# Moving the softmax division of two attention mixers from the probabilities to the stored outputs, and letting high-part splits run on GpSimd or ScalarE

## The chip, the cores and the metric

The kernel runs on one core of a Trainium2 chip. The metric is the device time of one execution in microseconds (us). A core has TensorE (PE in the rows, with its weight loads as PEld), VectorE (DVE), ScalarE (ACT), GpSimd (POOL) and SyncE (SP), which issues all transfers of this kernel.

## What is computed

A trunk of two layers on one sequence of 1024 tokens, width 1024, in float32. Each layer:

```python
h = rmsnorm(x, ln1_g[layer]);  proj = h @ w_in[layer]          # 2464 columns
out_a = mixer_dilated(...)   # A: 6 heads of 64, three dilated windows, softmax
out_b = mixer_mla(...)       # B: 6 heads of 64 (query/key 96), low-rank q and kv, softmax
out_c = mixer_diff(...)      # C: 4 heads, softmax1 - lambda * softmax2, sub-norm
x = x + concat([out_a, out_b, out_c]) @ w_o[layer]
x = x + square(relu(rmsnorm(x, ln2_g[layer]) @ w_up[layer])) @ w_down[layer]
# after both layers: rmsnorm(x, final_g)
```

In each head of A and B, `p = softmax(scores + mask)` over the keys and `out = p @ v`. All attention is causal.

## The kernel before

**Precision.** Every product of two float32 tensors is made of three TensorE products: each operand is split into a high part (`hi`, a rounded copy) and a low part (`lo`, the operand minus its high part), and high*high, high*low and low*high are summed in PSUM (`mm3`). The high part is a copy: `hi_pool` (kind `hi`, from SBUF) or `hi_act` (kind `hiact`, from PSUM). The low part is a subtraction (`lo_dve`, `lo_pool`).

**The scheduler.** The program is not written in the order in which it runs. Every instruction is noted by `Recorder`, and `order` then runs a list scheduler over the notes with costs in ns for each engine; each engine gets its instructions in the order that this planner found, and works through them strictly in that order. Tiles come from tags with a fixed number of slots (`SLOTS`; `'pp'` has 5, `'ms'`, `'mx'` and `'oo'` have 2 each), and an instruction is planned when a slot is free. Where `WAYS` names several letters for a kind of work (v VectorE, s ScalarE, g GpSimd), the planner picks the engine. All instructions of the kernel carry the line of the replay loop (L418), so in the rows the tile names tell them apart.

**The attention of a layer.** There are 16 heads in the order A0, C0, C1, A1, A2 (two heads each) and then six heads of B. `scores` handles 8 blocks of 128 queries of a head: TensorE makes the scores (`s_A`, `s_B`), VectorE adds the mask and takes the row maximum (`p_A`, with the maximum in `w_A`), ScalarE takes the exponential in place and its row sum, and for A and B

```python
nc.vector.reciprocal(w[:, 3:4], tot)     # VectorE, 128x1
copy("norm", p, p, w[:, 3:4])            # GpSimd, the block's 128 to 1024 columns
```

`values` then transposes the block on TensorE (`ptp_A`), splits it on ScalarE and VectorE (`ph_A`, `pl_A`) and multiplies it with the values (`o_A`, which holds two partial sums in its two halves of 64 partitions). `o_sum` copies both halves to SBUF on ScalarE (`ot_A`, `od_A`), adds them on GpSimd and stores 64x512 to `mix_dram`. Beside the heads run the other products of the layer as side work: the projections of the next heads (`pf_C`, `pf_A`, whose weights are split into `wh` and `wl`), latent products of B, and the output projection (`po`) of the 128-row groups of the mixed outputs in the order (6, 0), (7, 1), (2, 3, 4), (5).

**The end of the attention.** `project_load` reads each 128x512 half of a group's mixed outputs back from `mix_dram` (`mixr`, tag `'pp'`), splits it into `mixh` (GpSimd) and `mixl`, and splits the weights of the projection (`h_wo`, `l_wo`). Groups 2, 3, 4 and then 5 come after the last head. The first eight PSUM banks of that last projection belong to tokens 0 to 511, which need only the first half (`z` = 0) of each group. The feed-forward part follows.

## Time and profile before

| what | value |
|---|---|
| time, median of 3 runs | 2548.02 us (2547.39 to 2551.18) |
| time of the profiled execution | 2549.46 us |
| its span | 2547.7 us |
| PE busy | 2473.8 us (97%) |
| DVE busy | 2069.9 us (81%) |
| ACT busy | 1238.3 us (49%) |
| POOL busy | 920.2 us (36%) |
| mean granted clock of TensorE | 0.991 |

The span is what the profile sees from the first to the last instruction; the execution's own time is 1.8 us longer. Matmuls are pipelined and their ends are modelled, so a busy PE can hide short waits. The shares are means over two layers with two kinds of stages: attention (about 60 to 640 us and 1340 to 1920 us) and feed-forward.

### The profile page before, as it was taken

The numbers are of one execution on the slowest core, as the hardware profiler recorded it, in microseconds if no ns is written. First come the engines' busy times: TensorE is split into PE (matmuls) and PEld (weight loads), VectorE is DVE, ScalarE is ACT, GpSimd is POOL, SyncE is SP. The second block draws the span as 40 slices with busy tenths as digits, with TensorE's granted clock in tenths as the row PEclk, the third lists the DMA queues.
The fourth block names the chain that finished last, engine by engine and source line by source line (L and its number), as shares of the span: only waits on it lengthen the run. The fifth ranks groups of instructions, "written<-read, shape, count | busy, mean of one in ns | idle before, by whom it ended". The sixth has DMA issues, their size and how long they took to land. (4 is left out here: it accounts for less than half of the span.)

```text
span 2547.7 us, 39227 instructions
## 1 busy us (share of the span) xinstructions
PE 2473.8 (97%) x12808; PEld 2077.0 (82%) x12808; DVE 2069.9 (81%) x4326; ACT 1238.3 (49%) x2548; POOL 920.2 (36%) x1078
## 2 busy tenths in 40 slices
PE   8999999999999999999999999999999999999996
PEld 7878889988788887888888778898887888788885
DVE  4679998887877777989856799988778777789989
ACT  3566667743544444323235666677345444333332
POOL 2344355653200114455323343556330001144543
PEclk9999999999999999999999999999999999999998
DMA  8354433433354457544453554344243444765332
GB/s 255 96 142 135 112 94 94 135 93 130 116 172 164 153 197 262 156 145 120 137 164 97 133 137 122 81 110 142 78 142 129 163 159 146 268 210 157 112 120 79
DMA packets 292636, 360.58 MB, mean 142 GB/s; under 512 B 48848, under 2 KB 172112, under 8 KB 292432
## 3 DMA queue, kind: packets, MB, share of 16 engines
q1 hardware_dynamic: 292432, 358.08, 45.6%
q8 instruction: 102, 1.67, 0.3%
q14 instruction: 102, 0.84, 0.1%
HBM read 231.63 MB, written 94.90 MB: 128 GB/s over the span
## 5 line engine op out<-in xcount | busy, mean ns | idle before, releaser
L418 PE MATMUL pd<-hb,ha 128*128 128x512 f32 x2520 | 577.2, 390 | 5.4 <-DVE hb L418 3.5
L418 PE MATMUL pu<-xc,uh 128*128 128x512 f32 x1792 | 552.7, 393 | 13.4 <-ACT ua L418 8.2
L418 PEld LDWEIGHTS pd<-hb,ha 128*128 128x128 f32 x2520 | 471.4, 188 | 109.6 <-DVE hb L418 8.3
L418 PEld LDWEIGHTS pu<-xc,uh 128*128 128x128 f32 x1792 | 336.9, 189 | 90.0 <-ACT ua L418 10.0
L418 PE MATMUL pu<-xc,ul 128*128 128x512 f32 x896 | 346.7, 393 | 0.0
L418 PEld LDWEIGHTS pu<-xc,ul 128*128 128x128 f32 x896 | 169.6, 189 | 36.8 <-DVE ul L418 0.8
L418 DVE TENSOR_TENSOR ha<-hr,ha 128x512 fp32r<-128x512 f32 x151 | 145.6, 967 | 24.8 <-POOL ha L418 23.0
L418 POOL TENSOR_SCALAR ha<-hr 128x512 fp32r<-128x512 f32 x90 | 74.1, 824 | 245.1 <-DVE xd L418 94.8
L418 ACT ACTIVATE hb<-wt 128x512 fp32r<-128x512 f32 x98 | 60.4, 627 | 184.4 <-PE pd L418 157.3
L418 ACT ACTIVATE uh<-su 128x512 fp32r<-128x512 f32 x124 | 77.5, 631 | 138.4 <-PE pu L418 121.6
L418 ACT ACTIVATE hb<-wd 128x512 fp32r<-128x512 f32 x82 | 50.4, 627 | 158.8 <-PE pd L418 157.3
L418 ACT ACTIVATE p_C<-p_C,w_C 128x256 f32<-128x256 f32 (+7 forms) x128 | 98.9, 773 | 55.3 <-DVE w_C L418 54.7
L418 POOL TENSOR_SCALAR p_A<-p_A,w_A 128x128 f32<-128x128 f32 (+3 forms) x96 | 77.2, 806 | 116.5 <-DVE w_A L418 83.6
L418 POOL TENSOR_SCALAR uh<-wu 128x512 fp32r<-128x512 f32 x16 | 13.3, 832 | 280.1 <-PE pu L418 168.5
L418 DVE TENSOR_TENSOR hb<-wt,hb 128x512 fp32r<-128x512 f32 x105 | 109.7, 1061 | 0.7 <-ACT hb L418 0.5
L418 DVE TENSOR_TENSOR xd<-pd,xd 128x512 f32<-128x512 f32 x128 | 86.8, 682 | 26.6 <-PE pd L418 26.5
L418 PE MATMUL pf_C<-wh_C,hh 128*128 128x512 f32 x256 | 104.7, 413 | 1.7 <-POOL wh_C L418 0.9
L418 PE MATMUL pf_C<-wl_C,hh 128*128 128x512 f32 x256 | 104.4, 408 | 0.4 <-DVE wl_C L418 0.3
L418 PE MATMUL po<-h_wo,mixh 128*128 128x512 f32 x256 | 103.3, 403 | 1.0 <-POOL h_wo L418 1.0
L418 POOL TENSOR_SCALAR p_B<-p_B,w_B 128x384 f32<-128x384 f32 (+4 forms) x96 | 74.4, 780 | 79.8 <-DVE w_B L418 62.3
L418 PE MATMUL pf_A<-wh_A,hh 128*128 128x512 f32 (+1 forms) x256 | 100.0, 395 | 3.0 <-DVE w_C L418 2.1
L418 PE MATMUL pf_C<-wh_C,hs_C 128*128 128x512 f32 x256 | 101.8, 401 | 0.7 <-DMA hs_C<-hl_dram 0.7
(343 smaller groups left out, 6775.8 us busy)
## 6 DMA issues: line engine op xcount, KB each, us to landing
hr<-hc_dram SPq DMA_DIRECT2D x210, 256.0 KB, 2.8
wu<-in_w_up_dram SPq DMA_DIRECT2D x148, 256.0 KB, 3.0
hc_dram<-hc SPq DMA_DIRECT2D x120, 256.0 KB, 2.3
wd<-in_w_down_dram SPq DMA_DIRECT2D x120, 256.0 KB, 3.7
hs_C<-hl_dram SPq DMA_DIRECT2D x32, 512.0 KB, 3.5
hs_A<-hl_dram SPq DMA_DIRECT2D x32, 512.0 KB, 3.5
hc_dram<-ua SPq DMA_DIRECT2D x60, 256.0 KB, 2.3
hl_dram<-hl SPq DMA_DIRECT2D x16, 512.0 KB, 5.6
```

The costliest lines, as they stand in the source:

```text
L418: getattr(getattr(self.nc, eng), method)(*[real(v) for v in args], **{k: real(v) for k, v in kw.items()})
```

## The change

For A and B the probabilities are no longer divided. The row sums of the exponentials go into one 128x8 tile per head (`sums`, a column per block of queries). After blocks 3 and 7 TensorE transposes four columns of it to a 4x128 row tile in PSUM (`pts`), VectorE takes its reciprocal (`rs`), and it is stored as a row of 512 in `rs_dram`. The head's product `o` is copied once, 128x512, and both halves are stored apart in `half_dram`, not added. `project_load` reads the two halves (`mixr`, now tag `'ms'`, and `mixo`, tag `'mx'`) and the row of reciprocals twice, spread over 64 partitions each (`mixs`, tag `'pp'`), adds the halves and multiplies by the reciprocals on VectorE or GpSimd (kind `onorm`), and then splits as before. Apart from that the kind `hi` may now run on ScalarE as well as on GpSimd. C is computed as before, except that its `hi` splits have that choice too.

```diff
 LAG = 3
 DEEP = 6000.0
 
-WAYS = {'hi': 'g', 'hiact': 's', 'lo': 'vg', 'lop': 'g', 'evac': 'sv', 'norm': 'g', 'osum': 's', 'oadd': 'g', 'lsc': 'gs', 'rope': 'v', 'sq': 's', 'fadd': 'gv', 'fhi': 'sg', 'flo': 'vg', 'fnorm': 'sg', 'fevac': 'sv', 'fsnap': 's', 'fsq': 'sv'}
+WAYS = {'hi': 'gs', 'hiact': 's', 'lo': 'vg', 'lop': 'g', 'evac': 'sv', 'onorm': 'vg', 'osum': 's', 'oadd': 'g', 'lsc': 'gs', 'rope': 'v', 'sq': 's', 'fadd': 'gv', 'fhi': 'sg', 'flo': 'vg', 'fnorm': 'sg', 'fevac': 'sv', 'fsnap': 's', 'fsq': 'sv'}
 SHARED = 0.5
 
 BLOCKS = (0, 4, 8, 12, 15)
@@ -522,6 +522,8 @@
     hl_dram = nc.tile(dram, [DEPTH * NT, P, D], F32, "hl_dram")
     cq_dram = nc.tile(dram, [DEPTH * S, 512], F32, "cq_dram")
     mix_dram = nc.tile(dram, [DEPTH * D, S], F32, "mix_dram")
+    half_dram = nc.tile(dram, [2, DEPTH * 6 * P, S], F32, "half_dram")
+    rs_dram = nc.tile(dram, [DEPTH * 12, S], F32, "rs_dram")
 
     def rstd_of(y, ssq, n, eps, w, nm):
 
@@ -822,13 +824,18 @@
                                                scalar=w[:, 0:1] if z else BIG, op0=ALU.add, op1=ALU.min, accum_out=w[:, z:z + 1])
                 if c0 + m < W:
                     return
-                tot = hd["tot"][mi][:, i] if "tot" in hd else w[:, 2:3]
+                tot = hd["tot"][mi][i] if coef is None else hd["tot"][mi][:, i]
                 nc.scalar.activation(p, p, AF.Exp, bias=w[:, z:z + 1], scale=-1.0, accum_out=tot)
                 if mi == 0:
-                    if coef is None:
-                        nc.vector.reciprocal(w[:, 3:4], tot)
-                        copy("norm", p, p, w[:, 3:4])
                     hd["P"][g][i % 2] = p
+                    if coef is None and i % 4 == 3:
+
+                        z = i // 4
+                        pt = bank("c", f"pts_{nm}_{z}")
+                        nc.tensor.transpose(pt[:4, 0:P], hd["sums"][:, 4 * z:4 * z + 4], ident)
+                        r = tl("oo", [4, P], f"rs_{nm}_{z}")
+                        nc.vector.reciprocal(r, pt[:4, 0:P])
+                        nc.sync.dma_start(rs_dram[hd["row"], z * 512:z * 512 + 512].rearrange("(t p) -> t p", p=P), r)
                 else:
 
                     prev = hd["P"][g][i % 2]
@@ -893,15 +900,25 @@
 
             tmp = tl("oo", [P, 512], f"ot_{nm}_{g}")
             rows = slice(64 * par, 64 * par + 64)
-            dst = tl("oo", [P, 512], f"od_{nm}_{g}")[rows, :] if f < 6 else mix_tile(f, g)[rows, :]
+            dst = mix_tile(f, g)[rows, :]
             copy("osum", tmp[rows, :], o[64:128, :])
             copy("osum", dst, o[0:64, :])
             pair("oadd", dst, dst, tmp[rows, :], ALU.add)
-            if f < 6:
-                mix_out(f, g, dst, 64 * par, 64)
 
         def fin_mix(f, par, nm):
-            return lambda g, o: o_sum(g, o, f, par, nm)
+            def fin(g, o):
+
+                tmp = tl("oo", [P, 512], f"ot_{nm}_{g}")
+                copy("osum", tmp, o)
+                for z in range(2):
+                    r = (L * 6 + f) * P + 64 * par
+                    nc.sync.dma_start(half_dram[z, r:r + 64, g * 512:(g + 1) * 512], tmp[64 * z:64 * z + 64, :])
+            return fin
+
+        def summed(h, f):
+
+            t = one([P, NT], "sums")
+            return dict(sums=t, tot=[[t[:, i:i + 1] for i in range(NT)]], row=(L * 6 + f) * 2 + h % 2)
 
         def mask_a(W, c0, m):
             return maska[:, S - W + c0:S - W + c0 + m]
@@ -936,7 +953,7 @@
             q = turned(f"q{nm}", two(qa), lambda cs, pt: hi_act(qs[:, cs], pt))
             bl = zipped(k[0], k[1], q[0], q[1])
             return bl, dict(maps=[([(qs, k1s), (qs, k2s)], None)], mask=mask_a, scale=SC_A, nm=nm, P={},
-                            v=make_v(va[:, :, c], par, nm), fin=fin_mix(i, par, nm))
+                            v=make_v(va[:, :, c], par, nm), fin=fin_mix(i, par, nm), **summed(h, i))
 
 
         bx = {}
@@ -1082,7 +1099,7 @@
             qh, ql = [z[:96] for z in pairs[i][0][j]]
             kh, kl = [Halves(*z) for z in pairs[i][1][j]]
             return [], dict(maps=[([(qh, kh), (qh, kl), (ql, kh)], None)], mask=mask_c, scale=SC_B, nm=nm, P={}, cut=512,
-                            v=make_v(bx["V"][:, :, 64 * h:64 * h + 64], j, nm), fin=fin_mix(3 + i, j, nm))
+                            v=make_v(bx["V"][:, :, 64 * h:64 * h + 64], j, nm), fin=fin_mix(3 + i, j, nm), **summed(h, 3 + i))
 
         cst = {}
 
@@ -1208,8 +1225,19 @@
                 ml = tl(tag, [P, S], f"mixl_{L}_{f}", F32R)
                 for z in range(2):
                     cs = slice(z * 512, (z + 1) * 512)
-                    raw = tl("pp", [P, 512], f"mixr_{L}_{f}_{z}")
-                    nc.sync.dma_start(raw, mix_dram[L * D + f * P:L * D + (f + 1) * P, cs])
+                    raw = tl("ms", [P, 512], f"mixr_{L}_{f}_{z}")
+                    if f < 6:
+                        r = slice((L * 6 + f) * P, (L * 6 + f + 1) * P)
+                        nc.sync.dma_start(raw, half_dram[0, r, cs])
+                        other, rs = tl("mx", [P, 512], f"mixo_{L}_{f}_{z}"), tl("pp", [P, 512], f"mixs_{L}_{f}_{z}")
+                        nc.sync.dma_start(other, half_dram[1, r, cs])
+                        for j in range(2):
+                            src = rs_dram[(L * 6 + f) * 2 + j:(L * 6 + f) * 2 + j + 1, cs]
+                            nc.sync.dma_start(rs[64 * j:64 * j + 64, :], src.broadcast_to([64, 512]))
+                        pair("onorm", raw, raw, other, ALU.add)
+                        pair("onorm", raw, raw, rs, ALU.mult)
+                    else:
+                        nc.sync.dma_start(raw, mix_dram[L * D + f * P:L * D + (f + 1) * P, cs])
                     hi_pool(mh[:, cs], raw)
                     lo_dve(ml[:, cs], raw, mh[:, cs])
                 mx.append((mh, ml))
```

The planner's result differs all over the program. Counted over the program, GpSimd has 1083 instructions before and 655 after, ScalarE 2126 and 2260, VectorE 4328 and 4238, TensorE 12810 and 12858, and SyncE issues 1503 and 1671 transfers. Of the weight splits of the projections, ScalarE now has 30 of 32 `wh_C`, 22 of 32 `wh_A` and 6 of 16 `wh`; of the 48 additions and multiplications of kind `onorm`, 44 are on VectorE. In all 190 splits of kind `hi` are now on ScalarE.

**GpSimd, at the end of the second head of A** (`p_A_7` is its last block of queries; `tm_kC`, `tm_qC` and `vhl_C` are the splits with which the first C head begins, `wh_C` are weight splits of the next projection). Before:

```order
L418 TENSOR_SCALAR p_A_7_0_1469<-p_A_7_0_1469,w_A_7_0_1470 128x1024
L418 TENSOR_TENSOR tm_qC_1_1571<-qkv_C_713,tm_qC_1_1571 128x4x32
L418 TENSOR_SCALAR wh_C_5_1590<-wr_C_5_1458,g_73 128x512
L418 TENSOR_SCALAR tm_qC_1_1571<-qkv_C_713 128x4x32
L418 TENSOR_SCALAR wh_C_6_1605<-wr_C_6_1555,g_73 128x512
L418 TENSOR_TENSOR tm_qC_1_1571<-qkv_C_713,tm_qC_1_1571 128x4x32
L418 TENSOR_SCALAR tm_kC_0_1629<-qkv_C_713 128x4x32
L418 TENSOR_SCALAR tm_kC_1_1637<-qkv_C_713 128x4x32
L418 TENSOR_TENSOR tm_kC_0_1629<-qkv_C_713,tm_kC_0_1629 128x4x32
L418 TENSOR_TENSOR tm_kC_1_1637<-qkv_C_713,tm_kC_1_1637 128x4x32
L418 TENSOR_SCALAR tm_kC_0_1629<-qkv_C_713 128x4x32
L418 TENSOR_SCALAR vhl_C_1668<-qkv_C_713 128x8x64
```

After:

```order
L418 TENSOR_SCALAR tm_kC_1_1558<-qkv_C_724 128x4x32
L418 TENSOR_TENSOR tm_kC_1_1558<-qkv_C_724,tm_kC_1_1558 128x4x32
L418 TENSOR_TENSOR tm_kC_0_1556<-qkv_C_724,tm_kC_0_1556 128x4x32
L418 TENSOR_SCALAR tm_kC_1_1558<-qkv_C_724 128x4x32
L418 TENSOR_SCALAR tm_kC_0_1556<-qkv_C_724 128x4x32
L418 TENSOR_TENSOR tm_kC_1_1558<-qkv_C_724,tm_kC_1_1558 128x4x32
L418 TENSOR_TENSOR tm_kC_0_1556<-qkv_C_724,tm_kC_0_1556 128x4x32
L418 TENSOR_TENSOR tm_qC_0_1565<-qkv_C_724,tm_qC_0_1565 128x4x32
L418 TENSOR_SCALAR vhl_C_1621<-qkv_C_724 128x8x64
L418 TENSOR_TENSOR vhl_C_1621<-qkv_C_724,vhl_C_1621 128x8x64
```

The division of the block and all three weight splits are gone from between the splits of the C head.

**ScalarE, at the same place** (`ph_A` is the high part of the transposed probabilities, `ks_C` and `qs_C` are copies of keys and queries out of PSUM). Before:

```order
L418 ACTIVATE p_A_6_0_1424,w_A_6_0_1425<-p_A_6_0_1424,w_A_6_0_1425 128x896
L418 ACTIVATE ph_A_2_0_1488<-ptp_A_2_0_1396 128x512
L418 ACTIVATE p_A_7_0_1469,w_A_7_0_1470<-p_A_7_0_1469,w_A_7_0_1470 128x1024
L418 ACTIVATE ph_A_2_1_1513<-ptp_A_2_1_1416 128x512
L418 ACTIVATE ph_A_2_2_1523<-ptp_A_2_2_1440 128x384
L418 ACTIVATE ks_C_1449<-pt_kC_1_1567 128x512
L418 ACTIVATE qs_C_1583<-pt_qC_0_1574 128x512
```

After:

```order
L418 ACTIVATE ph_A_2_0_1453<-ptp_A_2_0_1398 128x512
L418 ACTIVATE wh_C_4_1461<-wr_C_4_1378,g_73 128x512
L418 ACTIVATE p_A_6_0_1418,sums<-p_A_6_0_1418,w_A_6_0_1419 128x896
L418 ACTIVATE ph_A_2_1_1477<-ptp_A_2_1_1413 128x512
L418 ACTIVATE tm_kC_1_1489<-qkv_C_724 128x4x32
L418 ACTIVATE ph_A_2_2_1500<-ptp_A_2_2_1451 128x384
L418 ACTIVATE tm_qC_0_1491<-qkv_C_724 128x4x32
L418 ACTIVATE tm_kC_1_1489<-qkv_C_724 128x4x32
L418 ACTIVATE tm_qC_1_1493<-qkv_C_724 128x4x32
L418 ACTIVATE wh_C_5_1529<-wr_C_5_1411,g_73 128x512
L418 ACTIVATE p_A_7_0_1483,sums<-p_A_7_0_1483,w_A_7_0_1484 128x1024
L418 ACTIVATE ks_C_1440<-pt_kC_1_1534 128x512
```

The weight splits `wh_C_4` and `wh_C_5` now stand directly ahead of the exponentials of blocks 6 and 7, and splits of the C head stand between.

**VectorE, after the last head of B** (groups 3, 4 and 5 of the mixed outputs on the way to the last projection). Before:

```order
L418 TENSOR_TENSOR mixl_3_7803<-mixr_3_0_7728,mixh_3_7774 128x512
L418 TENSOR_TENSOR mixl_3_7803<-mixr_3_1_7737,mixh_3_7774 128x512
L418 TENSOR_TENSOR l_wo_4_0_7819<-r_wo_4_0_7617,h_wo_4_0_7788 128x512
L418 TENSOR_TENSOR mixl_4_7825<-mixr_4_0_7744,mixh_4_7800 128x512
L418 TENSOR_TENSOR l_wo_4_1_7836<-r_wo_4_1_7645,h_wo_4_1_7821 128x512
L418 TENSOR_TENSOR mixl_4_7825<-mixr_4_1_7777,mixh_4_7800 128x512
L418 TENSOR_TENSOR mixl_5_7852<-mixr_5_0_7798,mixh_5_7831 128x512
L418 TENSOR_TENSOR mixl_5_7852<-mixr_5_1_7813,mixh_5_7831 128x512
```

After:

```order
L418 TENSOR_TENSOR mixr_3_0_7714<-mixr_3_0_7714,mixo_3_0_7445 128x512
L418 TENSOR_TENSOR mixr_3_0_7714<-mixr_3_0_7714,mixs_3_0_7663 128x512
L418 TENSOR_TENSOR mixr_3_1_7729<-mixr_3_1_7729,mixo_3_1_7492 128x512
L418 TENSOR_TENSOR mixr_3_1_7729<-mixr_3_1_7729,mixs_3_1_7676 128x512
L418 TENSOR_TENSOR mixl_3_7784<-mixr_3_0_7714,mixh_3_7768 128x512
L418 TENSOR_TENSOR l_wo_5_0_7790<-r_wo_5_0_7744,h_wo_5_0_7781 128x512
L418 TENSOR_TENSOR mixl_3_7784<-mixr_3_1_7729,mixh_3_7768 128x512
L418 TENSOR_TENSOR l_wo_5_1_7805<-r_wo_5_1_7755,h_wo_5_1_7798 128x512
L418 TENSOR_TENSOR mixr_4_0_7793<-mixr_4_0_7793,mixo_4_0_7760 128x512
L418 TENSOR_TENSOR mixr_4_0_7793<-mixr_4_0_7793,mixs_4_0_7698 128x512
L418 TENSOR_TENSOR mixr_4_1_7808<-mixr_4_1_7808,mixo_4_1_7778 128x512
L418 TENSOR_TENSOR mixr_4_1_7808<-mixr_4_1_7808,mixs_4_1_7709 128x512
```

Each half of a group has an addition and a multiplication ahead of its low part, and group 4 begins only behind both low parts of group 3, whose slots in `'ms'` its own tiles take.

## Rows read from the trace of the kernel before

**Rows 1.** The page, first part: busy time in us of each engine, its share of the span, and its instructions.

```profile
PE 2473.8 (97%) x12808; PEld 2077.0 (82%) x12808; DVE 2069.9 (81%) x4326; ACT 1238.3 (49%) x2548; POOL 920.2 (36%) x1078
```

**Rows 2.** Busy time by stretch. Columns: the stretch in us from the span's start, its length, then busy us and instructions of PE, PEld, DVE, ACT and POOL, the mean granted clock of TensorE, the busy share of the DMA engines and the GB/s they moved. The first two stretches are the attention of the two layers, the third lies in the feed-forward part, the last two are the densest parts of the attention.

```profile
64.00:640.00 576.00, 560.21 (x3416) 484.37 (x3416) 472.77 (x1312) 348.06 (x796) 267.35 (x361) 0.99 0.41 115
1344.00:1920.00 576.00, 562.58 (x3432) 485.38 (x3431) 475.37 (x1327) 352.47 (x791) 264.35 (x355) 1.00 0.40 115
704.00:896.00 192.00, 192.00 (x847) 158.11 (x846) 146.95 (x221) 87.40 (x144) 11.76 (x12) 1.00 0.48 162
192.00:384.00 192.00, 183.98 (x1100) 159.18 (x1099) 176.71 (x543) 124.37 (x291) 86.66 (x119) 0.98 0.41 114
1472.00:1664.00 192.00, 184.05 (x1155) 159.69 (x1153) 178.22 (x546) 127.58 (x294) 92.70 (x133) 0.99 0.40 110
```

**Rows 3.** The waits of TensorE over the whole span, as engine and tile <- what it waited for: us in total, times, longest us.

```profile
PE pt_kA L418 <- POOL tm_kA L418: 5.7, 3, 2.2
PE s_A L418 <- DVE w_A L418: 1.4, 1, 1.4
PE ptp_A L418 <- POOL p_A L418: 1.5, 3, 0.8
```

**Rows 4.** Busy time by stretch (columns as in rows 2) for the four short stretches of the attention in which the granted clock fell.

```profile
66.00:74.00 8.00, 5.77 (x21) 4.23 (x20) 7.44 (x11) 3.28 (x13) 3.95 (x7) 0.79 0.56 163
158.00:166.00 8.00, 6.17 (x23) 4.90 (x24) 5.02 (x24) 4.87 (x18) 2.04 (x6) 0.79 0.90 257
373.00:385.00 12.00, 9.46 (x52) 8.19 (x51) 10.74 (x24) 6.94 (x14) 8.92 (x12) 0.72 0.38 80
1630.00:1638.00 8.00, 6.23 (x35) 4.85 (x33) 7.41 (x15) 4.71 (x9) 7.20 (x9) 0.79 0.44 94
```

**Rows 5.** The timeline of GpSimd from 369 us and TensorE's answer to it, in order of time. Columns: start us, us, engine, line, operation, out<-in, partitions x elements out<-in, how many, and in brackets the idle time before it and what ended that.

```profile
369.85 1.23 POOL L418 TENSOR_SCALAR p_A<-p_A,w_A 128x640 f32<-128x640 f32 x1
373.54 1.27 POOL L418 TENSOR_TENSOR od_A<-od_A,ot_A 64x512 f32<-64x512 f32 x1 [1.32 <-issue]
374.88 0.73 POOL L418 TENSOR_TENSOR tm_kA<-qkv_A,tm_kA 128x256 fp32r<-128x256 f32 x1
375.66 0.66 PE L418 MATMUL pt_kA<-ident,tm_kA 128*128 128x128 f32 x4 [1.77 <-POOL tm_kA L418]
```

**Rows 6.** The same for GpSimd from 146 us, and TensorE behind it.

```profile
147.24 1.12 POOL L418 TENSOR_SCALAR wh_C<-wr_C,g 128x512 fp32r<-128x512 f32 x1
156.57 1.28 POOL L418 TENSOR_TENSOR od_A<-od_A,ot_A 64x512 f32<-64x512 f32 x1
159.83 1.43 PE L418 MATMUL s_C<-ks_C,qs_C 128*128 128x256 f32 x6 [1.96 <-issue]
```

**Rows 7.** The costliest groups of the page (part 5) and of the groups by shape, GpSimd: line, engine, operation, out<-in, shapes, count | busy us, mean ns | idle time before them and what ended it.

```profile
L418 POOL TENSOR_SCALAR p_A<-p_A,w_A 128x128 f32<-128x128 f32 (+3 forms) x96 | 77.2, 806 | 116.5 <-DVE w_A L418 83.6
L418 POOL TENSOR_SCALAR p_B<-p_B,w_B 128x384 f32<-128x384 f32 (+4 forms) x96 | 74.4, 780 | 79.8 <-DVE w_B L418 62.3
L418 POOL TENSOR_TENSOR od_B<-od_B,ot_B 64x512 f32<-64x512 f32 x24 | 32.4, 1351 | 23.6 <-ACT od_B L418 16.8 <-issue 5.0 <-POOL mixh L418 1.3
L418 POOL TENSOR_TENSOR od_A<-od_A,ot_A 64x512 f32<-64x512 f32 x24 | 31.5, 1311 | 15.4 <-ACT od_A L418 7.6 <-issue 5.1 <-PE ptp_B L418 1.3
```

**Rows 8.** Groups by shape on VectorE (columns as in rows 7).

```profile
L418 DVE RECIPROCAL w_B<-w_B 128x1 f32<-128x1 f32 x96 | 15.1, 157 | 9.0 <-ACT p_B L418 8.5
L418 DVE RECIPROCAL w_A<-w_A 128x1 f32<-128x1 f32 x96 | 14.8, 155 | 15.3 <-ACT p_A L418 14.8
L418 DVE RECIPROCAL ci<-tot 128x8 f32<-128x8 f32 x8 | 1.5, 188 | 0.0
L418 DVE TENSOR_TENSOR xr<-po,xr 128x512 f32<-128x512 f32 x96 | 65.1, 685 | 38.4 <-PE po L418 38.0
L418 DVE TENSOR_TENSOR mixl<-mixr,mixh 128x512 fp32r<-128x512 f32 x32 | 27.8, 902 | 0.0
```

**Rows 9.** Groups by shape on TensorE (columns as in rows 7).

```profile
L418 PE MATMUL pd<-hb,ha 128*128 128x512 f32 x2520 | 577.2, 390 | 5.4 <-DVE hb L418 3.5 <-ACT hb L418 1.5 <-DVE ha L418 0.3
L418 PE MATMUL pf_C<-wh_C,hh 128*128 128x512 f32 x256 | 104.7, 413 | 1.7 <-POOL wh_C L418 0.9 <-ACT cqj L418 0.8
L418 PE MATMUL pf_C<-wl_C,hh 128*128 128x512 f32 x256 | 104.4, 408 | 0.4 <-DVE wl_C L418 0.3
L418 PE MATMUL pf_C<-wh_C,hs_C 128*128 128x512 f32 x256 | 101.8, 401 | 0.7 <-DMA hs_C<-hl_dram 0.7
L418 PE MATMUL ptkr<-ident,ks 128*64 128x128 f32 x16 | 2.1, 274 | 0.7 <-POOL ks L418 0.7
```

**Rows 10.** Groups by shape on ScalarE (columns as in rows 7).

```profile
L418 ACT ACTIVATE uh<-wu 128x512 fp32r<-128x512 f32 x80 | 50.4, 630 | 102.9 <-PE pu L418 91.4 <-PE po L418 4.6 <-DMA wu<-in_w_up_dram 3.6
L418 ACT ACTIVATE ot_B<-o_B 64x512 f32<-64x512 f32 x24 | 14.3, 594 | 20.9 <-PE o_B L418 20.8
```

**Rows 11.** The waits of GpSimd for a transfer, over the whole span (columns as in rows 3).

```profile
POOL wh_C L418 <- DMA wr_C<-in_w_in_dram: 21.9, 7, 9.6
POOL wh_A L418 <- DMA wr_A<-in_w_in_dram: 19.5, 16, 2.8
```

**Rows 12.** The page, part 6: a transfer by what it moves, count, KB each, median us from issue to landing; then the transfer queue's timeline (columns as in rows 5) at the end of the first layer's attention.

```profile
mixr<-mix_dram SPq DMA_DIRECT2D x32, 256.0 KB, 3.4
584.01 3.11 SPq L418 DMA_DIRECT2D mixr<-mix_dram  x5
```

## The prediction

> **What bounds the kernel now.** I read the shares first: TensorE is busy for 97% of the span, the next engine for 81% [rows 1]. So a gain must come out of TensorE's idle time or its clock, and the stretches show where these are. In the feed-forward part TensorE has no idle time at all: 847 matmuls of 512 columns in 192 us, or 0.227 us each [rows 2]. In the attention it idles for 15.8 us in the first layer and 13.4 us in the second (576 less the busy time), and in the densest 192 us of each, where VectorE is busy for 92%, for 8 us [rows 2]. A pipelined matmul also hides short waits. The projection `pf_C` shows them: its three forms last 413, 408 and 401 ns where the feed-forward part's `pd` lasts 390 [rows 9], so 256 x (23 + 18 + 11) ns = 13 us of hidden lateness in this group alone.
>
> Then the waits by name. `pt_kA` waits 5.7 us for GpSimd's `tm_kA`, `ptp_A` 1.5 us for the divided block `p_A`, `s_A` 1.4 us for VectorE [rows 3]. The timeline tells why: at 369.85 us GpSimd divides a block, at 373.54 it adds two halves of an output, and only then, at 374.88, comes the low part that TensorE stands still for until 375.66 [rows 5]. At 147 to 157 us it is the same with weight splits and an addition, and TensorE starts the first C head at 159.83 after 1.96 us of nothing [rows 6]. After such waits the granted clock falls from full speed (2.4 GHz) to half (1.2 GHz) for some us: four short stretches show means of 0.79, 0.79, 0.72 and 0.79 [rows 4]. Their idle time is 2.2 + 1.8 + 2.5 + 1.8 = 8.4 us, and the missing clock is worth 0.21 x 8 x 3 + 0.28 x 12 = 8.4 us.
>
> **What the change removes, GpSimd.** 192 divisions (77.2 + 74.4 us) and 48 additions (32.4 + 31.5 us) leave it, 216 us of its 920 [rows 1, 7]; 190 high-part splits go to ScalarE besides. In the rows of the order, the division, the weight splits and the addition that delayed the C head are gone. What can come back is the 16.8 us of rows 4, and some 3 us at the same place in the second layer, where the first C head also starts late: 20 us at most. I take 13 us, two thirds, because the subtractions of the C heads stay on GpSimd in the same number; the bounds are 0 (another engine is late at the same place) and 20.
>
> **VectorE.** 192 reciprocals of one column go (15.1 + 14.8 = 30 us), and with them 14.8 + 8.5 = 23 us in which VectorE, whose queue is in order, stood waiting for the exponential [rows 8]. 48 reciprocals of 4x128 come. No row has that shape. One column takes 0.157 us and eight take 0.188 [rows 8], so 4.4 ns a column and 0.157 + 127 x 0.0044 = 0.72 us, 35 us in all; the lower bound is the eight-column price, 9 us. I take 35, since a length of 128 is nearer to the slope than to the start. VectorE's dense stages thus lose 18 us of work and waiting on balance. The Trainium skill (VectorE: DVE Perf Modes, "First, the fixed hardware budget") says that a reciprocal is an iterated divide with a repeat count of 8. At the 0.96 GHz of its title page (Trainium Kernel Development and Optimization, "NeuronCore Architecture") that would be an estimated 1.07 us for 128 columns and 51 us in all, which is 16 us more than by the rows; the slope of the row is about half of that rate.
>
> 44 additions and multiplications of the outputs also land on VectorE: 0.685 us each by `xr`, 0.902 by `mixl`, which has both operands in SBUF [rows 8], so 30 to 40 us. They fall into the output projection, the sparser end of the attention, where TensorE is the longer engine. GpSimd's smaller load should also stretch VectorE's SBUF operations less. How much of all this reaches TensorE is the open term: the bounds are 0 (TensorE was hidden behind something else) and the 13 us of hidden lateness. I take 7 us.
>
> **What it adds, TensorE.** 48 transposes of the sums, each on the engine that is the bound. `ptkr`, with the same 128 columns through half the array, takes 2.1 us for 16 [rows 9], 0.13 us each: +6 us. The lower bound is 0, where they fill a gap.
>
> **ScalarE.** 96 copies of a half of an output (0.594 us [rows 10]) become 48 of the same length, -29 us; 190 splits at up to 0.63 us [rows 10] come, at most +120 us. ScalarE is busy for 60% of the attention (348 of 576 us [rows 2]) and has the room. But it is in order too: GpSimd waited 21.9 us for `wr_C` and 19.5 for `wr_A` [rows 11], and now most of those waits stand ahead of exponentials. I take +1 us; the bounds are 0 and 10, a quarter of the 41 us.
>
> **The end of the attention.** Before, the tiles of groups 2 to 5 had five slots, and five reads went out together at 584 us [rows 12]. Now there are two. The read of a half of group 4 waits until group 3's low part is done, so groups 3, 4 and 5 go in rounds: read 3.4 us [rows 12], addition and multiplication 0.69 each, high part 0.63, low part 0.69 to 0.90 [rows 8, 10], together 6.1 to 6.3 us and with the handovers near 7. TensorE has 24 matmuls for each group in its eight banks, 24 x 0.227 = 5.4 us. Each round is then about 1 to 1.6 us late, after a first one that is covered by group 2 and the rest of group 1. For three rounds I take +2.5 us a layer, +5 in all; bounds 0 (more work of group 1 covers it) and +12 (the queue of transfers, at 3.11 / 5 = 0.62 us an issue [rows 12], adds its own lateness to each round, and TensorE's clock falls as in rows 4). What waits behind them on VectorE are the additions that free the eight banks.
>
> The Trainium skill (DMA: Bandwidth & Descriptors, "Rules for kernel authors") speaks against two transfers to the two halves of the partitions, because they share the same engines, and wants one of 128. The change does that with the stores and with the rows of reciprocals, and it issues 168 more transfers in all. By the 0.62 us of rows 12 these are 104 us of a queue that is spread over two attentions of 576 us; no run here yet shows whether any of them is waited for, and the sum holds them only through the end of the attention.
>
> **The sum.** -13 (GpSimd and the clock) - 7 (VectorE) + 6 (TensorE) + 1 (ScalarE) + 5 (end) = -8 us against the profiled execution's 2549.5 us, so 2541.5. The median of the runs is 1.4 us below that execution, which puts the forecast at 2540 us.
>
> **Rivals.**
> 1. *More comes back.* All 20 us of rows 4 and their twin and the whole 13 us of VectorE's lateness return, and half of the transposes fill gaps: -20 - 13 + 3 + 1 + 5 = -24, about 2524 us. For it: GpSimd stands at the head of each of these waits. Against it: C heads have no division, so the densest stage keeps most of its work.
> 2. *The change does not do what it says for the time.* What GpSimd loses was waited for in few places, ScalarE takes over the lateness, and a relief of 10 us is paid back by 6 + 1 + 5 us of costs: about 2550 us. For it: only 7 us of named waits end on GpSimd [rows 3].
> 3. *The end turns the sign.* Two slots make rounds of 7.5 us and more. Each is then 2 us late and after 1 to 2 us of idle time the clock falls, a spell of about 3 us at half speed: 6 + 2 us a layer, 16 in all; with transposes and ScalarE (6 + 1) and the small relief of rival 2 that is +13, about 2561 us. It decides from rounds of about 8 us on, against 5.4 us of matmuls. For it: nothing but the last groups is left for TensorE there. Against it: `z` = 1 halves are not needed at once.
> 4. *ScalarE's order.* Splits that wait for a transfer hold back exponentials and high parts of transposed blocks, which feed TensorE directly: +10, with transposes and rounds (6 + 5) and half of the relief (-10 to -13) about 2557 us. For it: the order puts `wh_C` ahead of the exponentials. Against it: ScalarE idles for two fifths of the attention [rows 2].
>
> **How the numbers follow.** The forecast's own range is 2530 to 2548: the two terms of relief together between 14 and 26 us (I take 20), the costs between 8 and 14 (I take 12). Chances: forecast 45%, more 15%, no change 18%, the end 13%, ScalarE 9%. A change under 0.2%, 5.1 us, could not be told from none here. Faster means under 2543: 36 of the forecast's 45 points and rival 1 give 0.51. The other 9 points and 16 of rival 2's 18 give 0.25 for no change, and the slower rivals with the last 2 points give 0.24. For 8 times in 10 the range runs from 2518 to 2561; it leaves out the far half of each outer case.
>
> **What would show it.** Right: GpSimd near 550 us busy, no wait of `pt_kA` for `tm_kA`, a clock without the four falls of rows 4, `pf_C` closer to 390 ns, reciprocals of 4x128 near 0.7 us. Wrong: waits of `po` for `mixh` or VectorE above 3 us a layer at the end of the attention, with a new fall of the clock; exponentials behind `wh_C` that waits for a transfer; transposes `pts` that TensorE waits for. The prediction fails if the lateness of TensorE in the attention was set by the data dependences of a head rather than by the load of GpSimd and VectorE, or if the new order of the whole program happens to leave other gaps.

## The result and the profile after

The changed kernel is slower: 2567.42 us (median of 4 runs, 2565.16 to 2568.44), a ratio to the kernel before of 1.0072 with a 95% interval of 1.0052 to 1.0091. By this ratio that is some 18 us (the two medians lie 19.4 us apart); the forecast was 2540 us, its own range 2530 to 2548 us, and the range for 8 times in 10 ended at 2561 us. One execution of the kernel before (5947.85 us) and one of run 10 below (3087.55 us) stand far off all others of their kernels and enter no ratio. The profiled execution took 2567.27 us, its span is 2565.5 us. The first lines are the page's busy shares [answering rows 1], then stretches [rows 2]; the last two stretches are the ends of the two attentions.

```profile
PE 2477.8 (97%) x12856; PEld 2083.4 (81%) x12856; DVE 2080.9 (81%) x4236; ACT 1295.0 (50%) x2682; POOL 582.4 (23%) x650
```

```profile
64.00:640.00 576.00, 551.63 (x3380) 476.26 (x3379) 469.34 (x1238) 362.96 (x840) 109.43 (x157) 0.99 0.46 129
192.00:384.00 192.00, 184.58 (x1096) 158.83 (x1096) 170.29 (x532) 131.30 (x310) 48.54 (x68) 0.99 0.41 117
576.00:640.00 64.00, 59.69 (x286) 48.26 (x286) 49.01 (x103) 26.95 (x50) 7.89 (x13) 0.95 0.56 177
1856.00:1920.00 64.00, 58.23 (x259) 47.00 (x258) 47.83 (x113) 28.39 (x55) 9.88 (x15) 0.92 0.59 184
```

The same two ends in the kernel before:

```profile
576.00:640.00 64.00, 62.98 (x319) 52.19 (x318) 46.89 (x107) 25.20 (x48) 22.57 (x29) 1.00 0.40 138
1856.00:1920.00 64.00, 63.57 (x312) 52.74 (x311) 49.30 (x134) 36.39 (x71) 20.54 (x26) 1.00 0.37 128
```

GpSimd lost 338 us of its 920 and VectorE gained 11. In the densest 192 us VectorE is busy 6 us less and GpSimd 38 us less, and TensorE got nothing for it (184.58 us against 183.98). At the ends TensorE idles for 4.3 and 5.8 us of 64 where it idled for 1.0 and 0.4, and the granted clock falls to means of 0.95 and 0.92, as it does between full speed and half after waits [rows 4].

TensorE's waits by name [rows 3], and the four short stretches of rows 4:

```profile
PE po L418 <- ACT mixh L418: 12.1, 9, 2.8
PE pt_kA L418 <- POOL tm_kA L418: 5.5, 1, 5.5
PE pf_C L418 <- ACT wh_C L418: 3.3, 2, 2.0
```

```profile
66.00:74.00 8.00, 2.46 (x9) 1.91 (x8) 5.74 (x11) 3.08 (x13) 6.26 (x5) 0.80 0.26 66
158.00:166.00 8.00, 6.98 (x34) 5.36 (x34) 6.37 (x27) 6.38 (x24) 0.00 (x0) 1.00 0.91 248
373.00:385.00 12.00, 9.77 (x59) 8.06 (x58) 11.70 (x27) 8.93 (x20) 6.40 (x10) 0.86 0.46 113
1630.00:1638.00 8.00, 7.08 (x48) 6.21 (x47) 6.53 (x14) 5.34 (x12) 3.77 (x4) 1.00 0.22 68
```

Three of the four falls of rows 4 are gone or smaller, as predicted; the first is worse (2.46 us of work in 8). But the projection waits 12.1 us for `mixh`, which was no wait at all before. Where the time is lost is plainest from two ends in each layer, the last matmul of the heads (`o_B`) and that of the output projection (`po`). First the kernel before, then the changed one, each for the first and then the second layer; after the count come min/median/max ns of one and the first and last start in us:

```profile
L418 PE MATMUL o_B<-ph_B,vhl_B x144: 220/280/392, 444.1 to 586.1; 128*128 128x256 f32 x96, 128*64 128x128 f32 x48
L418 PE MATMUL po<-h_wo,mixl x128: 387/389/483, 524.9 to 641.2; 128*128 128x512 f32 x128
L418 PE MATMUL o_B<-ph_B,vhl_B x144: 220/280/392, 1700.7 to 1842.4; 128*128 128x256 f32 x96, 128*64 128x128 f32 x48
L418 PE MATMUL po<-h_wo,mixl x128: 387/389/483, 1781.1 to 1897.3; 128*128 128x512 f32 x128
```

```profile
L418 PE MATMUL o_B<-ph_B,vhl_B x144: 218/281/387, 447.2 to 591.6; 128*128 128x256 f32 x96, 128*64 128x128 f32 x48
L418 PE MATMUL po<-h_wo,mixl x128: 387/392/628, 520.6 to 653.5; 128*128 128x512 f32 x128
L418 PE MATMUL o_B<-ph_B,vhl_B x144: 218/281/387, 1708.8 to 1854.1; 128*128 128x256 f32 x96, 128*64 128x128 f32 x48
L418 PE MATMUL po<-h_wo,mixl x128: 387/392/628, 1782.2 to 1918.6; 128*128 128x512 f32 x128
```

From the last start of `o_B` to that of `po` it took 55.1 and 54.9 us before, and 61.9 and 64.5 after: the ends cost 6.8 and 9.6 us (the expectations below count between the ends of the two, some 0.2 us more). At the last `o_B` the first layer was already 5.5 us late. The feed-forward parts give some of it back: the last `pd` of the first layer is only 7.3 us late after a projection that was 12.3 us late, and that of the second 17.8 us after 21.3, so they return 8.5 of the 16.4 us.

### The profile page after: what moved, and what is told of

Read it like the earlier page. It is cut to its first block, busy times and chain, and to the rows that moved or that the text cites. A ratio compares the mean times of both kernels' runs of the same rounds, so it can differ in the third digit from the quotient of the medians.

```text
span 2565.5 us, 38953 instructions
## 1 busy us (share of the span) xinstructions
PE 2477.8 (97%) x12856; PEld 2083.4 (81%) x12856; DVE 2080.9 (81%) x4236; ACT 1295.0 (50%) x2682; POOL 582.4 (23%) x650
## 5 line engine op out<-in xcount | busy, mean ns | idle before, releaser
L418 PE MATMUL pu<-xc,uh 128*128 128x512 f32 x1792 | 550.5, 392 | 11.8 <-ACT ua L418 6.9
L418 DVE TENSOR_TENSOR ha<-hr,ha 128x512 fp32r<-128x512 f32 x155 | 154.9, 1001 | 22.4 <-POOL ha L418 20.6
L418 PE MATMUL po<-h_wo,mixh 128*128 128x512 f32 x256 | 107.8, 421 | 12.1 <-ACT mixh L418 12.1
L418 PE MATMUL po<-l_wo,mixh 128*128 128x512 f32 x256 | 104.8, 410 | 0.0
L418 PE MATMUL po<-h_wo,mixl 128*128 128x512 f32 x256 | 101.4, 406 | 0.1
L418 PE MATMUL pf_A<-wl_A,hh 128*128 128x512 f32 (+1 forms) x256 | 98.9, 386 | 1.5 <-DVE wl_A L418 1.5
```

The costliest lines, as they stand in the source:

```text
L418: getattr(getattr(self.nc, eng), method)(*[real(v) for v in args], **{k: real(v) for k, v in kw.items()})
```

## The end of the attention in the trace

The transfer queue, VectorE, ScalarE and TensorE in the changed kernel, first layer (idle time before and what ended it in brackets):

```profile
595.58 2.28 SPq L418 DMA_DIRECT2D mixs<-rs_dram  x3
597.96 0.53 SPq L418 DMA_DIRECT2D mixr<-half_dram  x1
...
606.17 0.33 SPq L418 DMA_DIRECT2D mixr<-half_dram  x1
```

```profile
601.71 0.69 DVE L418 TENSOR_TENSOR mixr<-mixr,mixo 128x512 f32<-128x512 f32 x1 [2.60 <-DMA mixr<-half_dram]
602.44 0.69 DVE L418 TENSOR_TENSOR mixr<-mixr,mixs 128x512 f32<-128x512 f32 x1
...
605.46 0.68 DVE L418 TENSOR_TENSOR mixl<-mixr,mixh 128x512 fp32r<-128x512 f32 x1
...
611.67 0.69 DVE L418 TENSOR_TENSOR mixr<-mixr,mixo 128x512 f32<-128x512 f32 x1 [3.46 <-DMA mixr<-half_dram]
```

```profile
603.22 0.63 ACT L418 ACTIVATE mixh<-mixr 128x512 fp32r<-128x512 f32 x1 [7.64 <-DVE mixr L418]
```

```profile
604.00 0.77 PE L418 MATMUL po<-h_wo,mixh 128*128 128x512 f32 x1 [2.79 <-ACT mixh L418]
```

One half: read issued at 597.96, added at 601.71, multiplied at 602.44, high part at 603.22, TensorE starts at 604.00 after 2.79 us of nothing. Its low part ends at 606.14, only then does the slot take the next read (606.17), and that is added at 611.67. So this round was 10.0 us, not 7: from the issue of the read to the addition it took 5.5 us, where such a read had a median of 3.4 [rows 12], and other reads were under way. The next round took 6.6 us (its addition starts at 618.24), and the two of the second layer 10.7 and 6.7. And ahead of the first read stand reads of `mixs` that SP issues at 0.6 to 0.8 us each.

## Experiments

All ratios are to the kernel before, measured beside it (its medians there: 2548.4 to 2549.5 us), with 95% intervals. One hundredth of a per cent is 0.25 us. Runs 5, 11, 13, 14 and 15 leave out work that the result needs; they are there to price it.

**My theory after the result:** the two slots at the end cost most of it, and the rest is an order of the program that is a little less lucky. **Rivals:** ScalarE's queue with the splits (rival 4 of the prediction); a relief that never was; any new order.

**Run 1, more slots at the end.**
```diff
-                    raw = tl("ms", [P, 512], f"mixr_{L}_{f}_{z}")
+                    raw = tl("pw" if gi > 1 else "ms", [P, 512], f"mixr_{L}_{f}_{z}")
...
-                        other, rs = tl("mx", [P, 512], f"mixo_{L}_{f}_{z}"), tl("pp", [P, 512], f"mixs_{L}_{f}_{z}")
+                        other, rs = tl("ms" if gi > 1 and z else "mx", [P, 512], f"mixo_{L}_{f}_{z}"), tl("pp", [P, 512], f"mixs_{L}_{f}_{z}")
```


> The changed kernel, with one thing different: at the end of the attention (the last four features of the output projection) the first halves of the outputs are read into a tile with five slots, and the second halves alternate between two tiles of two slots, so that a read no longer waits for the low part of the half two before it. Theory of the end: the changed kernel loses 6.9 us at the end of the first attention (the last matmul of the projection moves from 641.6 to 653.9, of which 5.4 us were there before the end) and 9.6 us at the end of the second, because a round of read, addition, multiplication, high and low part takes 6.6 to 10 us on two slots. With the slots gone the waits of po for mixh fall from 12.1 us to under 3 us, and the time falls by 8 to 14 us, to 2553 to 2559 us. Rival, the transfers: the rounds are long because three transfers and their issues feed each half, whatever the slots; then po still waits over 8 us for mixh and the time stays at 2562 to 2569 us.

Measured: 2563.3 us, 1.0059 (1.0042 to 1.0075). The way from `o_B` to `po` shortens from 61.9 and 64.5 to 59.1 us in both layers, so half of the loss at the ends goes; but the feed-forward parts, from the last `po` to the last `pd`, take 5.7 us more together than in the changed kernel (where they were 607.1 and 607.8 us). The time gains 4 us. `po` still waits 5.6 us for `mixh` and 3.1 for `mixl`. Neither theory holds alone.

**Run 2, splits back on GpSimd** (`'hi': 'gs'` to `'hi': 'g'` in the changed kernel).


> The changed kernel with the high parts of splits on GpSimd alone, as before; divisions by rows stay. Theory of the end: the end of the attention is what costs most, and it does not depend on where high parts are split; po still waits 8 us or more for mixh, and the time is 2560 to 2572 us. Rival, ScalarE's order: the 190 splits on ScalarE hold back what feeds TensorE (pf_C and pf_A now wait 3.3 and 2.0 us for wh_C and wh_A on ScalarE); taking them off gives back 6 us or more, to 2553 to 2561 us.

Measured: 2568.9 us, 1.0083 (1.0066 to 1.0099); `po` waits 10.2 us, now for GpSimd's `mixh`. As the theory of the end has it; ScalarE's order as the main cause falls. The trace shows more than the time: with the two slots unchanged, the ends are 59.0 and 58.4 us, 9.0 us shorter together, but the feed-forward parts take 613.0 and 613.7 us, 11.8 us more. No run here asks why.

**Run 3, splits alone** (`'hi': 'g'` to `'hi': 'gs'` in the kernel before).


> The kernel before with one thing different: high parts of splits may go to ScalarE. No division by rows. Theory of the end: nothing at the end of the attention changes, so the time stays within 6 us of before, 2544 to 2556 us. Rival, ScalarE's order: slower by 6 us or more, over 2556 us. The reading of the prediction, that GpSimd's load holds TensorE back: faster by 5 us or more, under 2545 us, since about a fifth of GpSimd's work leaves it.

Measured: 2564.5 us, 1.0056 (1.0038 to 1.0073). A miss for my theory: this half of the change alone costs 14 us. It does not add up with run 2, so what a half costs depends on the rest of the kernel.

**Runs 4 and 8, the order alone** (`"sync": 200.0` to `"sync": 230.0` in the planner's table of handovers, in the kernel before and in the changed one).


> A control. The kernel before with the same work, slots and engines for everything; only the planner's guess of the time from a transfer's issue to its reader is 230 ns instead of 200, which draws another order of the whole program. If a new order by itself costs nothing, the time is within 3 us of before, 2546 to 2553 us. If the order of before is an unusually good one, so that any new one loses, it is 4 us or more slower, over 2553 us, and the 5 us that the changed kernel is late before the end of the attention need no other cause.

> A second control: the changed kernel with the planner's guess of a transfer's way to its reader at 230 ns instead of 200, which draws another order of the same work. If the 19 us belong to the change, it stays within 4 us of it, 2563 to 2571 us, with po still waiting 8 us or more for mixh; if a good part of them is an unlucky order, it comes out under 2560 us.

Measured: 1.0015 (1.0005 to 1.0025) and 1.0080 (1.0062 to 1.0098). Another order costs some 4 us in the one and 2 in the other (in the second the interval overlaps that of the changed kernel); most of the loss belongs to the change. And since every edit below draws a new order too, a difference of up to some 4 us between two kernels need not come from the edit.

**Run 5, no division at all** (the two lines `nc.vector.reciprocal(w[:, 3:4], tot)` and `copy("norm", ...)` taken out of the kernel before).


> The kernel before with the 192 reciprocals and the 192 multiplications of blocks on GpSimd left out and nothing in their place: the outputs of A and B heads are not divided by their sums. It prices the relief by itself, without transposes, rounds at the end or splits on ScalarE. The prediction's theory (GpSimd's and VectorE's load holds TensorE back; its two terms of relief, which it took at 20 us, hang on it): 12 to 25 us faster, 2523 to 2536 us. Theory of the data dependences (the chain from scores over minimum, exponential, transpose to output sets TensorE's lateness; a new order moves the waits elsewhere, as the order alone cost 3.6 us): between 6 us faster and 3 us slower, 2542 to 2552 us.

Measured: 2551.2 us, 1.0009 (0.9999 to 1.0019). This is the run that decides. The page's shares:

```profile
PE 2468.6 (97%) x12808; PEld 2076.2 (81%) x12808; DVE 2046.5 (80%) x4138; ACT 1235.0 (48%) x2538; POOL 773.3 (30%) x892
```

147 us of GpSimd and 23 us of VectorE are gone, nothing was added, and the time does not move. TensorE's busy time fell by 5.2 us, as if some hidden lateness had come back, but its idle time in the two attentions (576 less the busy time) rose from 15.8 and 13.4 us [rows 2] to 21.9 and 17.7:

```profile
64.00:640.00 576.00, 554.15 (x3413) 479.87 (x3412) 461.80 (x1218) 346.74 (x791) 194.81 (x268) 1.00 0.40 115
1344.00:1920.00 576.00, 558.28 (x3419) 483.63 (x3418) 462.63 (x1232) 349.10 (x784) 193.99 (x264) 1.00 0.40 115
```

Of the waits of rows 3, that of `pt_kA` falls from 5.7 to 2.2 us and that of `s_A` from 1.4 to 0.9; `ptp_A` waits 1.5 us as before, now for the exponential instead of the division. From 366 to 386 us, the place of rows 5, TensorE's named waits were 4.0 us together and are 4.2, mostly on other steps and other engines. The three longest of these, and then that of `ptp_A`:

```profile
PE ptl L418 <- ACT cc L418: 1.4, 1, 1.4
PE pt_qA L418 <- DVE pl_A L418: 1.3, 1, 1.3
PE ptl L418 <- POOL tm_kA L418: 0.6, 1, 0.6
PE ptp_A L418 <- ACT p_A L418: 1.5, 1, 1.5
```

**Run 11, VectorE in the heads** (in the kernel before, `parts[jp] = ph, ph` and no `pl`).


> The kernel before with the low parts of the transposed blocks left out on VectorE (the second matmul of each pair reads the high part again, so TensorE's work is the same; VectorE loses some 0.55 to 0.68 us for each block and the blocks need half as many slots). It asks what holds TensorE in the heads, since leaving out the divisions gave nothing. If VectorE is the bound there: 15 to 40 us faster, 2509 to 2534 us. If the chain from scores to outputs sets the lateness: within 8 us of before, 2541 to 2552 us.

Measured: 2542.7 us, 0.9972 (0.9959 to 0.9985). 167 us of VectorE's work buy 7 us:

```profile
PE 2460.7 (97%) x12808; PEld 2074.5 (82%) x12808; DVE 1902.9 (75%) x4017; ACT 1237.6 (49%) x2545; POOL 913.2 (36%) x1070
```

So neither engine's load alone is what TensorE waits for in the heads. Nor do these runs speak for the chain of a head's own steps: both shortened it (run 5 by a reciprocal of 0.16 us and a pass of 0.8 us over the block between exponential and transpose [rows 7, 8], run 11 by the subtraction between transpose and product) and got 0 and 7 us for it. A rival stays untested, that the two engines hold TensorE in turn. In run 11 TensorE waits 8.9 us for divided blocks, where it waited 1.5 before [rows 3]; no run left out both the division and the low parts.

```profile
PE ptp_A L418 <- POOL p_A L418: 8.9, 6, 2.0
```

**Run 6, rows for the A heads alone** (`summed` and `fin_mix` only for f < 3; B as before; splits on GpSimd).


> Sums stored as rows for the A heads only; the B heads, which end the attention, divide their blocks and add their halves on GpSimd as before and are read through five slots; high parts on GpSimd alone. The end of the attention is thus as before, with half of the transposes (24, some 2.7 us by the sum of matmul lengths) and most of the relief. If the end with its rounds and its queue of transfers is the main cost of dividing by rows (20 us by the second run, of which some 4 + 5 us lie at the ends), the time is 2548 to 2556 us. If the rows cost their time in the heads themselves, 2557 to 2566 us. By the prediction's theory of relief it would be faster than before, under 2543 us.

Measured: 2561.6 us, 1.0052 (1.0034 to 1.0071): a miss. The ends are cured (54.6 and 54.8 us from `o_B` to `po`), but `po` now waits 1.9 and 2.4 us for `mixh` in the middle of the B heads, at 528 and 1787 us, where the first group with rows is read, and at the last `o_B` both layers are 5 to 6 us late. The longer way is waited for there as well, though these 4.3 us are not the whole 13.

**Run 7, runs 1 and 2 together** (splits on GpSimd and the slots of run 1).


> Both single edits of the first two runs together: reads at the end through more slots, and high parts on GpSimd alone. If the two add up, 2568.9 - 4 = 2564 us; if ScalarE's queue was what kept the end late once the slots were gone (mixh there waits behind other work of ScalarE), 2553 to 2559 us, with po waiting under 3 us for mixh or mixl in both layers.

Measured: 2571.6 us, 1.0096 (1.0077 to 1.0114), no better than run 2: the ends stay at 58.8 and 59.9 us, and `po` waits 6.3 us for `mixh` and 3.2 for `mixl`.

**Runs 9 and 10, which splits** (in the kernel before a kind of its own for the three splits of weights: `'hi': 'gs', 'hiw': 'g'`, and the reverse).


> The kernel before with the high parts of splits free to go to ScalarE, except those of weights (wh, wh_A, wh_C, h_wo and the others that wait for a read of weights), which stay on GpSimd. Theory of ScalarE's order (a split that waits for a read of weights stands ahead of exponentials in ScalarE's queue): without them the 14 us of the third run shrink to 5 us or less, 2546 to 2554 us. If any shift of high parts to ScalarE costs, whatever they wait for, it stays at 2557 to 2566 us.

> The complement: only the high parts of weights may go to ScalarE, all others stay on GpSimd. Theory of ScalarE's order: this half holds the cost, 2557 to 2566 us, with ScalarE waiting for the reads wr_C and wr_A between exponentials. If the cost lies in the others, 2546 to 2554 us.

Measured: 1.0031 (1.0019 to 1.0044) and 1.0007 (0.9998 to 1.0017): the other way round. Splits that wait for weights on ScalarE cost nothing that can be told; rival 4 falls. The rest costs 8 us, and its largest new wait is `pt_kA` for `tm_kA`, 6.0 us. The changed kernel has the same wait (5.5 us, to 71.82). GpSimd and VectorE ahead of it in the changed kernel; in run 9 GpSimd's copy lasts 3.25 us too, from 66.54 on:

```profile
67.39 3.25 POOL L418 TENSOR_SCALAR tm_kA<-qkv_A 128x256 fp32r<-128x256 f32 x1 [5.31 <-ACT cqs L418]
70.73 1.03 POOL L418 TENSOR_TENSOR tm_kA<-qkv_A,tm_kA 128x256 fp32r<-128x256 f32 x1
```

```profile
67.15 1.09 DVE L418 TENSOR_TENSOR ru_A<-qkv_A,ropea 128x256 f32<-128x256 f32 x3
68.16 0.69 DVE L418 TENSOR_TENSOR qkv_A<-qkv_A,ropea 128x512 f32<-128x512 f32 x1
68.76 0.42 DVE L418 TENSOR_TENSOR ru_A<-qkv_A,ropea 128x256 f32<-128x256 f32 x1
69.09 0.69 DVE L418 TENSOR_TENSOR qkv_A<-qkv_A,ru_A 128x512 f32<-128x512 f32 x1
69.69 0.69 DVE L418 TENSOR_TENSOR qkv_A<-qkv_A,ropea 128x512 f32<-128x512 f32 x1
```

**Runs 16 and 17, the values' high part back on GpSimd** (`hi_pool(vh, vsrc)` kept on GpSimd, in run 9's kernel and in the changed one).


> The ninth run with one more kind kept on GpSimd: the high parts of the values (vhl). In every kernel in which they may go to ScalarE, TensorE waits 5.5 to 6.0 us for tm_kA at 66 to 72 us, where GpSimd's operation takes 3.25 us instead of 0.51 while VectorE works through seven operations on SBUF; in those without, the wait is 2.2 us. If that place is the cost of the ninth run (8 us), with the wait at 2.2 us the time falls to 2550 to 2554 us. If the cost is spread over the heads, it stays at 2555 to 2560 us.

> The changed kernel with only the high parts of the values (vhl) kept on GpSimd; everything else of the change stays. If the wait for tm_kA at 66 to 72 us is the cost of the splits in the changed kernel too, it falls from 5.5 to 2.2 us and the time falls by 3 to 6 us, to 2561 to 2565 us. If, with the divisions gone, the splits cost nothing more there (putting all of them back left the time at 2568.9), it stays at 2566 to 2570 us.

Measured: 1.0011 (1.0001 to 1.0022) and 1.0054 (1.0037 to 1.0071), 5 and 4.6 us less than without. The intervals overlap those without, and 4 us is also what another order can cost; the wait in the trace is clear, 2.2 us in both. GpSimd in run 16 (its next copy there is `tm_qA`, of the same shape), and TensorE's wait in run 17:

```profile
65.91 1.60 POOL L418 TENSOR_TENSOR vhl_A<-qkv_A,vhl_A 128x512 fp32r<-128x512 f32 x1
68.16 0.51 POOL L418 TENSOR_SCALAR tm_qA<-qkv_A 128x256 fp32r<-128x256 f32 x1 [0.64 <-DVE qkv_A L418]
```

```profile
PE pt_kA L418 <- DVE tm_kA L418: 2.2, 1, 2.2
```

One split that moved to ScalarE leaves GpSimd waiting for `tm_kA` alone, at the moment when VectorE has a run of operations on SBUF; the copy then lasts 3.25 us instead of 0.51. It lasts 3.25 us in all eight kernels in which this split may go to ScalarE (the changed one and runs 1, 3, 8, 9, 12, 13 and 14), and 0.51 in the nine in which GpSimd has it ahead of `tm_kA` (the kernel before and runs 2, 4, 5, 6, 7, 10, 11 and 15).

**Run 12, fewer issues at the end** (run 1, with `mixs` read for both halves at once into tag `'pw'` and `mixr` in `'pp'`).


> The first run once more with the queue of transfers relieved too: the rows of reciprocals are read for both halves at once (two transfers of 64x1024 for a feature instead of four of 64x512) into blocks that come free earlier, and the first halves of outputs at the end go back to the five slots that the kernel before used. If the 4 us a layer that were still left at the end in the first run were SP's queue, in which 16 issues of rows stood ahead of the last outputs from 588 to 598 us, the end is as early as before: the last matmul of the projection comes 55 to 57 us after the last one of the heads (55.2 in the kernel before, 62.1 in the changed one, 59.3 in the first run), and the time is 2554 to 2560 us. If the rounds are long because of the two more steps and reads, it stays at 2560 to 2566 us.

Measured: 2564.4 us, 1.0056 (1.0039 to 1.0073), 59.5 and 59.6 us from `o_B` to `po`. Fewer issues do not bring the end back: TensorE waits 3.5 us once in each layer, for a half that was read, added and multiplied.

**Run 13, no transposes of sums** (a store of `p[0:4, 0:P]` in place of `pts`, `rs` and its store).


> The changed kernel with the 48 transposes of sums and the 48 reciprocals of 4x128 left out; in their place four rows of a block of exponentials are stored as the row, so that transfers and waits for exponentials stay. It prices the transposes. If each costs TensorE its length, 0.11 us by the sum of lengths (2373.1 against 2367.8 us for the whole kernel), the time falls by 5 us, to 2560 to 2565 us. If they fill gaps, it stays within 3 us, 2565 to 2570 us.

Measured: 2562.7 us, 1.0049 (1.0034 to 1.0065), 6 us less than the changed kernel. (The two sums in the expectation add up the lengths of all matmuls, and no view here has them. The 0.11 us for a transpose of 128 columns can be seen where many follow each other: twelve `ptu` take 1.47 us in the kernel before, at 638.32 us.)

**Run 14, the short end** (`raw` in `'pp'`; `mixo`, `mixs` and both `onorm` lines taken out).


> The changed kernel with the end shortened to that of the kernel before: the second halves and the rows of reciprocals are not read, the addition and the multiplication are left out, and the first halves are read into five slots. Stores, transposes and splits stay. If the longer way from a stored output to TensorE (two slots, two more reads, an addition and a multiplication) is the cost of the end, the last matmul of the projection comes 55 to 57 us after the last one of the heads in both layers (62.1 and 64.7 in the changed kernel) and the time falls by 9 to 14 us, to 2553 to 2559 us. If the end is late for another reason (ScalarE has the high parts there, the stores of halves), it stays at 2561 to 2568 us.

Measured: 2558.9 us, 1.0035 (1.0021 to 1.0049), as the longer way expects:

```profile
L418 PE MATMUL o_B<-ph_B,vhl_B x144: 218/281/387, 447.6 to 593.3; 128*128 128x256 f32 x96, 128*64 128x128 f32 x48
L418 PE MATMUL po<-h_wo,mixl x128: 387/389/481, 526.6 to 649.9; 128*128 128x512 f32 x128
L418 PE MATMUL o_B<-ph_B,vhl_B x144: 218/281/387, 1704.9 to 1849.5; 128*128 128x256 f32 x96, 128*64 128x128 f32 x48
L418 PE MATMUL po<-h_wo,mixl x128: 387/389/482, 1783.8 to 1905.0; 128*128 128x512 f32 x128
```

56.6 and 55.5 us: both ends are back but for 1.5 and 0.6 us.

**Run 15, all three left out** (runs 13 and 14 together, `'hi': 'g'`).


> The changed kernel without the transposes and reciprocals, with the short end of the run above, and with all high parts on GpSimd as before: of the change only the removed divisions, the removed additions on GpSimd and the stores of halves and rows are left. If the three costs (transposes, end, splits) make up the whole difference and the relief is worth nothing, it is as fast as the kernel before and as the fifth run, 2545 to 2553 us. If the removed additions free TensorE after all, under 2543 us; if the stores cost something, over 2555 us.

Measured: 2548.7 us, 1.0003 (0.9989 to 1.0016). With transposes, longer end and splits gone, what is left of the change is as fast as the kernel before: the three together are the whole loss, and 208 us less on GpSimd are worth nothing (by the interval at most 2.8 us).

## Why the prediction was wrong

- **GpSimd, -13, and VectorE, -7: failed, measured 0 (runs 5 and 15).** The step was to read a wait as owned by the engine that ends it ("what can come back is the 16.8 us of rows 4"). Rows 4 did improve in three places, and in run 5 the waits for the division vanished, yet the time stayed (+2 us, -0.3 to +4.8): TensorE then waits for the next input, or a little later for another engine. Part of the reading was not in the rows at all: the wait of 1.96 us at 159.83 us ends on "issue" [rows 6], not on GpSimd, and it is 2.7 us in run 5, with the division gone. Nor did the hidden lateness go in the changed kernel: the forms of `pf_C` last 415, 407 and 406 ns, where they lasted 413, 408 and 401 [rows 9]. On the relief rival 2 came nearest ("waited for in few places"), with a weight of 18%, but it too left 10 us of it, to be paid back by 12 us of costs; on the time rival 3 did, at 2561 us and 13%, with 16 us at the ends.
- **VectorE's reciprocals, 35 us: measured 45.** The row below has 0.942 us for 128 columns, where the slope of eight columns gave 0.72 [rows 8]. The 1.07 us estimated from the Trainium skill (VectorE: DVE Perf Modes, "First, the fixed hardware budget") were nearer. With the 14.6 us of waiting in the row and 3.5 more for B, the 18 us that I took off VectorE were not there; run 11, where 167 us of VectorE bought 7, says that they would have bought nearly nothing.

```profile
L418 DVE RECIPROCAL rs_A<-pts_A 4x128 f32<-4x128 f32 x24 | 22.6, 942 | 14.6 <-PE pts_A L418 14.6
```

- **TensorE's transposes, +6: right in size.** Run 13 gives back 0.23 points, 6 us, though its interval overlaps that of the changed kernel.
- **ScalarE, +1: mis-sized, some 5 (runs 16 and 17, one order each), and for another reason.** It is not a split in ScalarE's queue that waits for weights (run 10) but one copy on GpSimd that now meets VectorE's operations on SBUF (runs 16 and 17). The prediction had no more for that than its last clause ("happens to leave other gaps").
- **The end, +5: right mechanism, mis-sized, 9.** Run 14 gives back 0.37 points, 9.4 us; in the trace the ends lose 6.8 + 9.6 = 16.4 us, of which the feed-forward parts return 8.5, a return that the prediction did not have. The rounds were 10.0 and 6.6 us in the first layer and 10.7 and 6.7 in the second where I took 7, mainly because the reads of the long rounds took 5.5 and 6.0 us among others, and rival 3's condition (rounds of about 8 us, with a new fall of the clock) was met. I gave the slots as the cause; run 1 shows that more slots take away half of the loss at the ends, and run 2 that the splits on GpSimd do so too with the slots as they are. The other half is left in runs 1, 2, 7 and 12 and goes only with the two more steps and reads (run 14).
- **The sum.** 0 + 6 + 5 + 9 = 20 us against 18 measured. That it comes so near is partly luck, since each term is a difference of two orders and the terms do not simply add up (runs 2, 3 and 7). Run 15 shows the three together. The main error is the relief.

What stays open: why the splits cost 14 us alone (run 3), beyond the one place found; why putting them all back (run 2) shortens the ends and lengthens the feed-forward parts; and what does set TensorE's 13 to 16 us of idle time in each attention. No variant that computes the whole result beats the kernel before. By the interval of run 5 removing the division brings 0.3 us at most in that one order; another order may move this by some 4 us (run 4).

## What to carry to other kernels

Price a relief before its replacement: one run that leaves the work out, and adds nothing, says what it can bring, up to the few us by which a new order alone moves the time. An engine that stands at the end of a wait need not own it, since a step with several inputs waits for the next one. And steps that are added between a stage's last result and the engine that is the bound are waited for there, even if the engine that does them idles (VectorE had 3.46 us of nothing to do before the addition at 611.67 us).
